# A two-layer decoder trunk: the last down group of the first layer in direct form

## The chip, the cores and the metric

The kernel runs on one core of a Trainium2 chip. The metric is the device time in microseconds (us) of one execution. Five engines work side by side, each through its own queue in order: TensorE (PE; PEld is its weight load), VectorE (DVE), ScalarE (ACT), GpSimd (POOL) and SyncE (SP), which here issues DMAs.

## The reference

512 tokens, 1024 features, two layers. Each layer adds an attention and an MLP to the residual x, all in float32:

```
for layer in range(2):
    h = rms_norm(x, g_mix[layer])
    x = x + even_mixer(...) if layer == 0 else x + odd_mixer(h, w_in_odd, b_forget, ...)
    h = rms_norm(x, g_mlp[layer])
    x = x + square(relu(h @ w_up[layer])) @ w_down[layer]
```

w_up is 1024 x 4096 and w_down 4096 x 1024. rms_norm divides each token by the root of its mean square and multiplies by a gain per feature. The odd mixer projects h to queries, keys, values (16 heads of 64) and 16 forget logits per token, whose cumulated log-sigmoid is added to the attention logits.

## The kernel before, in words

All is kept transposed: features on the 128 partitions, the 512 tokens along the free axis. The residual is four tiles `accs` of two feature chunks each. Every float32 product is made of three matmuls (`mm3`, L163 to L169): an operand is split into a rounded part (hi, a copy on ScalarE) and a remainder (lo, a subtraction on VectorE), and hi x hi, lo x hi and hi x lo are added up in PSUM.

The MLP (`mlp`, L730) works through `items`, and each item through positions. An up unit `("U", u)` computes 256 of the 4096 hidden features: four positions (two output halves by two halves of the input features) of 12 matmuls of 512 columns. A down group `("D", g, dp)` multiplies four finished units with one block of 256 output features. It uses a Strassen-like scheme of seven products (`ORDER`, L857): each operand is cut into 2 x 2 blocks, sums of blocks are formed for the weights (`ws`, L840) and for the units (`t_sums`, L773), and seven products of half width (256 columns) take the place of eight. Three of them add up in one bank, Y, from which VectorE adds into the residual after each product (`combine`, L923), and ScalarE copies the first product, X, into Y (L929). The items run: units 0 to 4, group 0, units 5 to 8, group 1, units 9 to 12, group 2, units 13 to 15, group 3.

In both layers the last group takes three units, and the last unit (`NL` = 1) is multiplied whole at the end: in the first layer chunk by chunk (L1052), six matmuls for each of the eight chunks. There each chunk is added to the residual (L1062), squared for the token sums of the next rms_norm (`squares`, L587; the adds of the first five on GpSimd, later ones on VectorE), scaled and split as the next layer's input (L1065), and stored to DRAM (L1068). `token_sums` (L596) then adds over the features by matmuls with ones, and `col_stats` (L137) makes the root's inverse `rcol`, a chain of small VectorE operations. The next layer's first projection (`vf_c`, L562: V of the first heads and the forget logits, 96 matmuls of 272 columns) uses the input without the token's scale; `forget` (L707) and V multiply by `rcol` after it.

The MLP's own rms_norm is applied late as well. `ssum` holds the mean square of each token; the residual is multiplied by it (`SCALE`, positions 12 to 18, L1002), the unscaled hidden features are squared and multiplied down, and near the end `ssum` is replaced by its reciprocal (L1006, position 4 of the last block of group 2) and the residual multiplied back (L1004), the last unit being scaled on its own (L950, GpSimd).

What sets the order: the loop at L1029 issues for each position its matmuls, the end of the position before, the split of weights six positions ahead (`prep`, R = 6), and what `todo` holds for that position (`at`, with the offsets in `FIN`, `FIND` and `FINL` after a unit, `plan`, L983). Weights are loaded eight positions ahead by SP (`early`, L860) into four buffers. Inside the MLP, VectorE, ScalarE, GpSimd and the first matmul of each step are held to program order (`pin`); elsewhere a planner orders each engine's queue by its own forecast of when operands are ready, with the program's order as priority. `load_w` (L179) loads and splits weights outside the items, on engines given by a pattern such as `PAT_ATT` (GpSimd, GpSimd and VectorE) or `PAT_START` (ScalarE and VectorE).

Of the kernel before, what the change touches and what calls it, by code (L numbers as in the profile page):

```python
# [9 lines left out]
F32 = mybir.dt.float32  # L10
# [34 lines left out]
XL = ((0, 0, 256), (0, 256, 512), (1, 0, 512), (1, 0, 0))  # L45
RPOS = (-8, 4)
SQP = 5
VENG = 'g'
SC2 = (11, 16, 26, 29)
SENG = ('vv', 'vv', 'vv', 'gg')  # L50
SENG_W = 'vvvv'
# [8 lines left out]
FIND = (0, 3, 7, 12, 17)  # L60
SCALE = (12, 14, 16, 18)
PINS = 'pgva'
TENG = 'vvvv'
# [10 lines left out]
def trunk(ctx, tc, x, g_mix, g_mlp, w_in_even, a_q_gain, a_k_gain, b_q_gain, b_k_gain, b_sinks,  # L74
# [117 lines left out]

    def layer_attention(li, hT, w_in, w_out):


        with ExitStack() as c2:
# [10 lines left out]

            def project(cols, use, ahead=False):

# [5 lines left out]
                for k0 in range(0, DC, kw):  # L215
                    srcs, o = [], 0
                    for a, b in cols:
                        srcs.append((0, o, w_in[k0 * P:(k0 + kw) * P, a:b]))
                        o += b - a
                    ws = load_w(srcs, w, kw, PAT_START if ahead else PAT_ATT)  # L220
                    if ahead:
# [288 lines left out]
            if li == 0:  # L510
                def qk_a(g):
                    return project([(g * 256, g * 256 + 256), (512 + g * 256, 512 + g * 256 + 256)], qk_use(g, 8), g == 0)

# [41 lines left out]
            else:  # L555
# [6 lines left out]
                def vf_c():  # L562
                    def use(outs):
                        forget(ap, outs)
                        v_use(0, 0)(outs)
                    return project([(2048, 2304), (3072, 3088)], use)

# [5 lines left out]

                all_of(vf_c())
                all_of(qk_c(0))
# [154 lines left out]
    def mlp(li, accs, attention_end, last):  # L730
# [5 lines left out]
        with ExitStack() as c2:  # L736
# [12 lines left out]
            def sca(m):  # L749
                pin("a", m)  # L750
# [56 lines left out]
            for g in range(NS):  # L807
                items.append(("U", 4 * g + 4))
                items += [("D", g, dp) for dp in range(4)]
                items += [("U", 4 * g + u) for u in range(5, 8)]  # L810
            items += [("D", NS, dp) for dp in range(4)]
            pos, first = [], []
            for j, it in enumerate(items):
                first.append(len(pos))
                pos += [(j, p) for p in range(4 if it[0] == "U" else 7)]
            NP = len(pos)
# [3 lines left out]
            def load(j):  # L820
                if j in raws or j >= len(items):
                    return
                it = items[j]
                raws[j] = [wp.tile([P, 4, 256], F32, tag="wraw", bufs=RAW, name="wraw") for _ in range(2)]
                for h in range(2):
                    if it[0] == "D":
                        src = wd[h, :, 4 * it[1]:4 * it[1] + nk(j), it[2] * 256:it[2] * 256 + 256]
                    else:
                        src = w_up[li, h * 512:(h + 1) * 512, it[1] * 256:it[1] * 256 + 256].rearrange(
                            "(k p) c -> p k c", p=P)  # L830
                    nc.sync.dma_start(raws[j][h][:, :nk(j)], src)

            def nk(j):

                return 4 - NL if items[j][:2] == ("D", NS) else 4

# [31 lines left out]
            def prep(n):  # L868
                if n >= NP:
                    return  # L870
                j, p = pos[n]
                if items[j][0] == "U":
                    src = quarter(j, (11, 12, 21, 22)[p])
                else:
                    i = ORDER[p][0]
                    src = quarter(j, i) if i > 10 else ws(j, i)
# [15 lines left out]
            def up_end(j, p):  # L892
                if p == 0:
                    res[j] = mp.tile([P, 2, 512], F32, tag="u", bufs=2, name="u")
                if p % 2:
                    sca(nc.scalar.activation(res[j][:, p // 2], res[j, p - 1], AF.Relu))  # L896

            def product(j, p, hi, lo):
# [36 lines left out]
            def unit_end(j):  # L935
# [7 lines left out]

                if u >= 16 - NL:
                    def whole(e):
                        s = slot("s")
                        halves(s[:, 0], s[:, 1], v[:, e])
                        store[u, e] = s

                    def scaled(e):  # L950
                        if not last:
                            scale(v[:, e], VENG)
                    return [square, lambda: scaled(0), lambda: scaled(1), lambda: whole(0), lambda: whole(1)]

# [28 lines left out]
            def plan(j):  # L983

                if items[j][0] == "D":
                    return
                u = items[j][1]
                n0 = first[j + 1]
                offs = FINL[u - 15 + NL] if u >= 15 - NL else FIND if u % 4 == 0 and u else FIN
                for i, f in enumerate(unit_end(j)):  # L990
                    at(n0 + offs[i], f)
# [9 lines left out]
            for dp in range(4):  # L1001
                at(SCALE[dp], lambda dp=dp: scale_residual(dp, SCENG[dp]))  # L1002
                if not last:
                    at(first[-4] + SC2[dp], lambda dp=dp: scale_residual(dp, SENG[dp]))  # L1004
            if not last:
                at(first[RPOS[0]] + RPOS[1], lambda: vec(nc.vector.reciprocal(ssum, ssum)))  # L1006

            def end(n):
                if n < 0:
                    return  # L1010
                j, p = pos[n]
                (up_end if items[j][0] == "U" else combine)(j, p)
                if n + 1 == NP or pos[n + 1][0] != j:
                    plan(j)

            early(0)
            npre = [0]
# [11 lines left out]
            for n, (j, p) in enumerate(pos):  # L1029
                early(n + R + LS)  # L1030
                hi, lo = ready.pop(n)
                (up if items[j][0] == "U" else product)(j, p, hi, lo)
                end(n - 1)
# [10 lines left out]
            ss = [store[u, e] for u in range(16 - NL, 16) for e in range(2)]  # L1044
            if last:
                down_last(li, accs, ss, r2col)
                return None

            ssum2 = mp.tile([P, 2, 512], F32, tag="u", bufs=2, name="ssum2")[:, 0]
            nh = []  # L1050
            r0 = FF // P - 2 * NL
            for c in range(DC):  # L1052
                if c % 4 == 0:
                    ws = []
                    for k in range(0, 2 * NL, 2):
                        ws += load_w([(0, 0, w_down[li, (r0 + k) * P:(r0 + k + 2) * P, c * P:(c + 4) * P])], 512, 2, PAT_MLP)
                o = bank("pB", "dn")
                cw = slice(c % 4 * P, c % 4 * P + P)
                for f in range(2 * NL):
                    mm3(o, ws[f][0][:, cw], ws[f][1][:, cw], ss[f][:, 0], ss[f][:, 1], f == 0, f == 2 * NL - 1, f == 0)  # L1060
                a = accs[c // 2][:, c % 2]
                nc.vector.tensor_add(a, o, a)  # L1062
                squares(c, a, ssum2, sq_pool, SQP)
                h = slot("hn")
                scale_split(h[:, 0], h[:, 1], a, gcol[:, 8 * (li + 1) + c:8 * (li + 1) + c + 1])  # L1065
                nh.append(h)
                if c % 2:
                    nc.scalar.dma_start(xsp[c // 2], accs[c // 2])  # L1068

            col_stats(token_sums(ssum2))  # L1070
            return nh

# [29 lines left out]
    accs, end = layer_attention(0, [], w_in_even[0], w_out_even[0])  # L1102
    hT = mlp(0, accs, end, False)
    accs, end = layer_attention(1, hT, w_in_odd[0], w_out_odd[0])
    mlp(1, accs, end, True)
# [22 lines left out]
```

## Time and profile before

| | us |
|---|---|
| median of 3 runs (lowest, highest) | 1203.42 (1201.02, 1204.06) |
| the profiled execution, its own time | 1202.71 |
| its span (first to last instruction) | 1200.7 |
| TensorE busy | 1165.1 |
| VectorE busy | 919.2 |
| ScalarE busy | 653.0 |
| GpSimd busy | 232.5 |

Busy times are of one execution. Durations of matmuls overlap, since they are pipelined; what a matmul costs TensorE is the distance from its start to the next one's. The granted clock (PEclk) is the share of TensorE's full clock of 2.4 GHz; the lower level is 1.2 GHz. The whole execution has a mean of 0.992.

### The profile page before, as it was taken

The page shows a single profiled execution, that of the slowest core. Times are in us where ns is not written, and L with a number is a line of the kernel's source. Part 1 is how long each engine was busy: PE and PEld are TensorE (multiplying, and loading weights), DVE is VectorE, ACT ScalarE, POOL GpSimd, SP SyncE. Part 2 cuts the span into 40 slices and gives each one's busy share as a digit, 9 for nine tenths or more (in the row PEclk, how much of TensorE's full clock was granted, in tenths as well). Part 3 has the DMA queues.
Part 4 walks back from the last instruction along what each step waited for, and adds up shares of the span by engine and source line. Part 5 has one row for each costly group of instructions (what it writes and reads, how often), then busy time and mean ns, then how long its engine had stood idle before and what let it go on. Part 6 is the DMA issues. An engine that isn't in the chain of part 4 may idle for free.

```text
span 1200.7 us, 19302 instructions
## 1 busy us (share of the span) xinstructions
PE 1165.1 (97%) x7014; PEld 1027.8 (86%) x7014; DVE 919.2 (77%) x2018; ACT 653.0 (54%) x1369; POOL 232.5 (19%) x327
## 2 busy tenths in 40 slices
PE   8799989999999999998899999999999999999998
PEld 7687887888988989988787888888889989989897
DVE  4887899868848858859947877778879668569575
ACT  6255876665545555445425675656755465455453
POOL 2445444200000000000755435332100000000000
PEclk9899999999999999999999999999999999999999
DMA  7342115232332332322543433343332422323322
GB/s 248 105 118 75 36 36 158 71 123 71 101 110 89 103 109 88 106 66 85 168 124 97 108 105 106 99 124 114 100 97 74 123 88 90 106 87 106 110 70 85
DMA packets 105718, 122.48 MB, mean 102 GB/s; under 512 B 6120, under 2 KB 94216, under 8 KB 105624
## 3 DMA queue, kind: packets, MB, share of 16 engines
q1 hardware_dynamic: 104440, 117.03, 32.6%
q0 software_dynamic: 576, 2.10, 0.5%
q10 hardware_dynamic: 608, 2.13, 0.4%
q8 instruction: 55, 0.90, 0.3%
q14 instruction: 39, 0.32, 0.1%
HBM read 108.10 MB, written 6.32 MB: 95 GB/s over the span
## 4 chain that ended last, share of the span: by engine, by line
PE 80%; DVE 10%; DMA 3%; issue 3%; POOL 2%; ACT 2%; SPq 0%; POOLq 0%; ACTq 0%; DVEq 0%
PE up L165 10%; PE up L168 10%; PE up L169 10%; PE pj L232 4%; PE pj L234 4%; PE pj L233 4%; PE Y L917 3%; PE Y L920 3%; PE Y L921 3%; PE O L383 3%; PE Z L917 2%; PE Z L921 2%; PE Z L920 2%; PE PT L363 2%; PE X L921 2%
## 5 line engine op out<-in xcount | busy, mean ns | idle before, releaser
L165 PE MATMUL up<-xin,whi 128*128 128x512 f32 x512 | 200.2, 391 | 0.0
L168 PE MATMUL up<-xin,wlo 128*128 128x512 f32 x512 | 199.7, 390 | 0.0
L169 PE MATMUL up<-xin,whi 128*128 128x512 f32 x512 | 199.5, 390 | 0.0
L759 DVE TENSOR_TENSOR wlo<-wraw,whi 128x512 fp32r<-128x512 f32 (+1 forms) x224 | 148.9, 675 | 64.3 <-ACT whi L758 59.9
L758 ACT CAST whi<-wraw 128x512 fp32r<-128x512 f32 (+1 forms) x224 | 135.3, 608 | 114.2 <-PE up L169 50.1
L758 ACT CAST whi<-s 128x512 fp32r<-128x512 f32 (+1 forms) x128 | 75.8, 593 | 76.2 <-PE Y L921 38.0
L169 PEld LDWEIGHTS up<-xin,whi 128*128 128x128 f32 x512 | 96.4, 188 | 20.2
L165 PEld LDWEIGHTS up<-xin,whi 128*128 128x128 f32 x512 | 96.5, 188 | 20.0 <-issue 0.2
L168 PEld LDWEIGHTS up<-xin,wlo 128*128 128x128 f32 x512 | 96.4, 188 | 20.0 <-issue 0.2
L917 PE MATMUL Y<-t,whi 128*128 128x256 f32 x360 | 103.2, 287 | 5.0 <-DVE acc L933 5.0
L920 PE MATMUL Y<-t,wlo 128*128 128x256 f32 x360 | 102.1, 284 | 0.0
L921 PE MATMUL Y<-t,whi 128*128 128x256 f32 x360 | 102.1, 284 | 0.0
L343 ACT ACTIVATE P<-P,negm 128x128 f32<-128x128 f32 (+5 forms) x128 | 69.6, 544 | 52.5 <-DVE negm L340 48.8
L153 POOL TENSOR_SCALAR whi<-wraw 128x512 fp32r<-128x512 f32 (+1 forms) x104 | 71.4, 690 | 122.0 <-PE pj L234 79.9
L896 ACT ACTIVATE u<-up 128x512 f32<-128x512 f32 x64 | 38.3, 599 | 101.9 <-PE up L169 101.9
L232 PE MATMUL pj<-whi,hn 128*128 128x512 f32 (+2 forms) x256 | 89.2, 348 | 0.0
L233 PE MATMUL pj<-wlo,hn 128*128 128x512 f32 (+2 forms) x256 | 87.6, 342 | 0.0
L234 PE MATMUL pj<-whi,hn 128*128 128x512 f32 (+2 forms) x256 | 87.4, 342 | 0.0
L759 DVE TENSOR_TENSOR wlo<-s,whi 128x512 fp32r<-128x512 f32 (+1 forms) x128 | 82.3, 648 | 3.1 <-ACT whi L758 3.1
L156 POOL TENSOR_TENSOR wlo<-wraw,whi 128x512 fp32r<-128x512 f32 (+1 forms) x56 | 73.4, 1314 | 21.0 <-ACT whi L151 17.8
L232 PE MATMUL pj<-whi,h 128*128 128x512 f32 (+1 forms) x192 | 68.3, 360 | 8.0 <-ACT sq L250 4.8
L917 PEld LDWEIGHTS Y<-t,whi 128*128 128x128 f32 x360 | 69.1, 192 | 6.1 <-DVE acc L933 5.8
(201 smaller groups left out, 3190.0 us busy)
## 6 DMA issues: line engine op xcount, KB each, us to landing
wraw<-in_w_up SPq DMA_DIRECT2D x64, 512.0 KB, 3.7
wraw<-in_w_down SPq DMA_DIRECT2D x52, 512.0 KB, 3.8
wraw<-in_w_in_odd SPq DMA_DIRECT2D x36, 256.0 KB, 3.0
K<-K SPq DMA_DIRECT2D x26, 256.0 KB, 2.9
wraw<-in_w_down SPq DMA_DIRECT2D x16, 384.0 KB, 3.7
wraw<-in_w_in_even SPq DMA_DIRECT2D x10, 512.0 KB, 3.7
wraw<-in_w_in_even SPq DMA_DIRECT2D x16, 256.0 KB, 4.5
xl<-xsp SPq DMA_DIRECT2D x8, 512.0 KB, 3.3
```

The source lines that it names most:

```text
L156: in_order((nc.gpsimd if lo == "pool" else nc.vector).tensor_sub(dst_l, src, dst_h.bitcast(F32)))
L165: m = nc.tensor.matmul(o, wh, xh, start=start, stop=False, skip_group_check=more)
L168: nc.tensor.matmul(o, wl, xh, start=False, stop=False, skip_group_check=more)
L169: nc.tensor.matmul(o, wh, xl, start=False, stop=stop, skip_group_check=more)
L232: nc.tensor.matmul(o, xh, hi[:, :n], start=k == 0, stop=False)
L233: nc.tensor.matmul(o, xh, lo[:, :n], start=False, stop=False)
L234: nc.tensor.matmul(o, xl, hi[:, :n], start=False, stop=k == DC - 1)
L758: sca(nc.scalar.copy(dst_h, src))
L759: late.append(lambda: vec(nc.vector.tensor_sub(dst_l, src, dst_h.bitcast(F32))))
L917: m = nc.tensor.matmul(o, wh, b(0), start=start, stop=False, skip_group_check=more)
L920: nc.tensor.matmul(o, wl, b(0), start=False, stop=False, skip_group_check=more)
L921: nc.tensor.matmul(o, wh, b(1), start=False, stop=stop, skip_group_check=more)
```

## The change

In the first layer the last group becomes four items of a new kind, `"E"`: a product of all four units (12 to 15) with a block of 256 output features in direct form, four positions of 12 matmuls of 512 columns. Its end (`direct_end`) finishes each chunk as soon as it is whole. Units 12 to 15 are not cut into blocks but squared, scaled by the reciprocal on VectorE and split whole (`part`), unit 15 in two halves as they come. The separate last unit is gone. `ssum` is inverted at position 22 (`RPL`), and the residual is multiplied back at positions 1, 3, 5 and 7 after the start of unit 13 (`SC3`), all on VectorE. The token sums and `col_stats` are handed to the next layer as a function, `stats`, which is called after three steps (`STATS`) of its first projection; that projection's weights are split on ScalarE and VectorE. The second layer's MLP stays as it was.

```diff
+FIN12 = (0, 5)
+RPL = 22
+SC3 = (1, 3, 5, 7)
+STATS = 3
...
-                    return project([(2048, 2304), (3072, 3088)], use)
+                    return project([(2048, 2304), (3072, 3088)], use, PAT_START)
...
-                all_of(vf_c())
+                g = vf_c()
+                for _ in range(STATS):
+                    next(g)
+                stats()
+                all_of(g)
                 all_of(qk_c(0))
...
-            items += [("D", NS, dp) for dp in range(4)]
+            items += [("D" if last else "E", NS, dp) for dp in range(4)]
...
-                pos += [(j, p) for p in range(4 if it[0] == "U" else 7)]
+                pos += [(j, p) for p in range(7 if it[0] == "D" else 4)]
...
-                return 4 - NL if items[j][:2] == ("D", NS) else 4
+                return 4 - NL if last and items[j][:2] == ("D", NS) else 4
...
+            def direct(j, p, hi, lo):
+
+                if p % 2 == 0:
+                    res[j, p] = bank(("pA", "pB")[j % 2], "dn")
+                o = res[j, p - p % 2]
+                for k in range(4):
+                    v = store[12 + k, p % 2]
+                    mm3(o, hi[:, k], lo[:, k], v[:, 0], v[:, 1], p % 2 == 0 and k == 0, bool(p % 2 and k == 3), k == 0)
+
+            def direct_end(j, p):
+
+                if p % 2 == 0:
+                    return
+                dp = items[j][2]
+                c = 2 * dp + p // 2
+                a = accs[dp][:, p // 2]
+                if c == 0:
+                    res["ssum2"] = consts.tile([P, 512], F32, tag="ssum", name="ssum2")
+                vec(nc.vector.tensor_add(a, res[j, p - 1], a))
+                h = slot("hn")
+                g = gcol[:, 8 * (li + 1) + c:8 * (li + 1) + c + 1]
+                sca(nc.scalar.activation(h[:, 0], a, AF.Copy, scale=g))
+                vec(nc.vector.scalar_tensor_tensor(h[:, 1], a, g, h[:, 0].bitcast(F32), op0=OP.mult, op1=OP.subtract))
+                squares(c, a, res["ssum2"], sq_pool)
+                hn.append(h)
+                if c % 2:
+                    nc.scalar.dma_start(xsp[dp], accs[dp])
...
+                def whole(e):
+                    s = slot("s") if u < 15 or last else mp.tile([P, 2, 512], F32R, tag="t24", bufs=2, name="s")
+                    halves(s[:, 0], s[:, 1], v[:, e])
+                    store[u, e] = s
...
+                def part(e):
+
+                    sca(nc.scalar.activation(v[:, e], v[:, e], AF.Square))
+                    scale(v[:, e], "v")
+                    whole(e)
+                    if u == 15:
+                        catch_up()
+
+                if not last and u >= 12:
+                    return [lambda: part(0), lambda: part(1)]
...
-                offs = FINL[u - 15 + NL] if u >= 15 - NL else FIND if u % 4 == 0 and u else FIN
+                if not last and u >= 12:
+                    offs = FIN12 if u == 12 else (0, 1)
+                else:
+                    offs = FINL[u - 15 + NL] if u >= 15 - NL else FIND if u % 4 == 0 and u else FIN
...
-                    at(first[-4] + SC2[dp], lambda dp=dp: scale_residual(dp, SENG[dp]))
+                    at(first[-7] + SC3[dp], lambda dp=dp: scale_residual(dp, "vv"))
             if not last:
-                at(first[RPOS[0]] + RPOS[1], lambda: vec(nc.vector.reciprocal(ssum, ssum)))
+                at(RPL, lambda: vec(nc.vector.reciprocal(ssum, ssum)))
...
+                if not last and items[j] == ("U", 15):
+                    if p % 2:
+                        unit_end(j)[p // 2]()
...
-            ssum2 = mp.tile([P, 2, 512], F32, tag="u", bufs=2, name="ssum2")[:, 0]
...
-            col_stats(token_sums(ssum2))
-            return nh
+            return hn, lambda: col_stats(token_sums(res["ssum2"]))
...
-    hT = mlp(0, accs, end, False)
-    accs, end = layer_attention(1, hT, w_in_odd[0], w_out_odd[0])
+    hT, stats = mlp(0, accs, end, False)
+    accs, end = layer_attention(1, hT, w_in_odd[0], w_out_odd[0], stats)
```

## Rows read from the trace of the kernel before

**Rows 1.** The page's first part: busy time, share of the span and instructions of each engine.

```profile
PE 1165.1 (97%) x7014; PEld 1027.8 (86%) x7014; DVE 919.2 (77%) x2018; ACT 653.0 (54%) x1369; POOL 232.5 (19%) x327
```

**Rows 2.** TensorE's waits between 440 and 640 us: who waited for whom, us in total, times, the longest.

```profile
PE Y L917 <- DVE acc L933: 5.0, 4, 1.9
PE pc L600 <- DVE ssum L594: 4.2, 1, 4.2
PE pz L715 <- DVE fz L711: 0.7, 1, 0.7
```

**Rows 3.** Windows of 10 us: busy us and instructions of each engine, granted clock, DMA share, GB/s.

```profile
500.00:510.00 10.00, 8.22 (x50) 7.52 (x49) 8.24 (x11) 2.60 (x5) 0.00 (x0) 0.83 0.36 105
...
550.00:560.00 10.00, 7.75 (x63) 7.35 (x62) 10.00 (x19) 4.56 (x10) 2.85 (x2) 1.00 0.30 92
...
590.00:600.00 10.00, 5.79 (x37) 5.58 (x37) 8.66 (x14) 2.16 (x4) 5.61 (x8) 0.76 0.51 161
```

**Rows 4.** The timeline of TensorE at the borders of the last group, the last unit, the first projection and the forget gate: start, us, engine, line, operation, output and inputs, idle time before and its releaser.

```profile
541.33 0.28 PE L910 MATMUL Y<-b,whi 128*128 128x256 f32 x1
...
576.16 0.40 PE L165 MATMUL dn<-s,whi 128*128 128x512 f32 x1
...
587.07 0.28 PE L232 MATMUL pj<-whi,hn 128*128 128x272 f32 x1
...
592.71 0.28 PE L232 MATMUL pj<-whi,hn 128*128 128x272 f32 x1
597.20 1.87 PE L600 MATMUL pc<-ones,ssum 128*128 128x1 f32 x8 [4.21 <-DVE ssum L594]
...
606.53 0.28 PE L234 MATMUL pj<-whi,hn 128*128 128x272 f32 x1
...
607.86 0.28 PE L715 MATMUL pz<-ident,fz 128*16 128x128 f32 x1 [0.75 <-DVE fz L711]
```

**Rows 5.** The timelines of VectorE and TensorE at the reciprocal, end of group 2 and start of unit 13.

```profile
501.88 3.35 DVE L1006 RECIPROCAL ssum<-ssum 128x512 f32<-128x512 f32 x1
...
503.50 0.28 PE L921 MATMUL X<-b,whi 128*128 128x256 f32 x1
505.56 0.39 PE L917 MATMUL Y<-t,whi 128*128 128x256 f32 x1 [1.78 <-DVE acc L933]
...
508.06 0.63 PE L168 MATMUL up<-xin,wlo 128*128 128x512 f32 x1
508.49 0.63 PE L169 MATMUL up<-xin,whi 128*128 128x512 f32 x1
...
510.03 0.39 PE L165 MATMUL up<-xin,whi 128*128 128x512 f32 x1
```

**Rows 6.** The timelines of VectorE and TensorE in group 0, around position 22 and in the block after it.

```profile
299.00 0.68 DVE L851 TENSOR_TENSOR s<-wraw 128x512 f32<-128x512 f32 x1
299.60 0.41 DVE L933 TENSOR_TENSOR acc<-Y,acc 128x256 f32<-128x256 f32 x1
...
310.61 0.42 DVE L933 TENSOR_TENSOR acc<-Y,acc 128x256 f32<-128x256 f32 x1
...
312.82 0.42 DVE L933 TENSOR_TENSOR acc<-Y,acc 128x256 f32<-128x256 f32 x1 [0.26 <-PE Y L921]
...
300.74 0.28 PE L917 MATMUL Y<-t,whi 128*128 128x256 f32 x1
...
301.46 0.28 PE L917 MATMUL Y<-t,whi 128*128 128x256 f32 x1
...
311.08 0.39 PE L917 MATMUL Y<-t,whi 128*128 128x256 f32 x1
```

**Rows 7.** The timelines of GpSimd and VectorE while GpSimd scales the last unit, and one VectorE operation of the same shape after it.

```profile
551.80 2.85 POOL L796 TENSOR_TENSOR u<-u,ssum 128x512 f32<-128x512 f32 x2 [319.87 <-ACT u L942]
...
551.94 1.58 DVE L759 TENSOR_TENSOR wlo<-wraw,whi 128x384 fp32r<-128x384 f32 x1
553.45 1.61 DVE L851 TENSOR_TENSOR s<-wraw 128x384 f32<-128x384 f32 x1
...
555.32 0.54 DVE L759 TENSOR_TENSOR wlo<-s,whi 128x384 fp32r<-128x384 f32 x1
```

**Rows 8.** The timeline of VectorE from the token sums to `rcol`, first and last and a long one, and TensorE's token sums in the second layer's MLP.

```profile
599.11 0.16 DVE L140 TENSOR_SCALAR msv<-pc 128x4 f32<-128x4 f32 x1 [1.30 <-PE pc L600]
...
601.21 1.14 DVE L134 TENSOR_TENSOR rsq<-rsq 128x4 f32<-128x4 f32 x1
...
606.12 0.16 DVE L135 SCALAR_TENSOR_TENSOR rcol<-rsq 128x4 f32<-128x4 f32 x1
...
883.15 0.95 PE L600 MATMUL pc<-ones,ssum 128*128 128x1 f32 x8
```

**Rows 9.** VectorE's groups between 251 and 588 us: line, operation, count, busy us and mean ns of one, idle before.

```profile
L794 DVE TENSOR_TENSOR acc<-acc,ssum 128x512 f32<-128x512 f32 x14 | 9.6, 722 | 0.0
...
L1062 DVE TENSOR_TENSOR acc<-dn,acc 128x512 f32<-128x512 f32 x6 | 4.0, 682 | 0.8 <-PE dn L169 0.8
```

**Rows 10.** VectorE's timeline at the first products of group 2.

```profile
467.23 0.42 DVE L933 TENSOR_TENSOR acc<-Z,acc 128x256 f32<-128x256 f32 x1 [0.56 <-PE Z L921]
```

**Rows 11.** TensorE's waits between 606 and 885 us, the longest.

```profile
PE S L326 <- DMA K<-K: 2.8, 3, 1.2
```

More of the change, by code (lines that the diff above doesn't have):

```diff
@@ L45 @@
 XL = ((0, 0, 256), (0, 256, 512), (1, 0, 512), (1, 0, 0))
-RPOS = (-8, 4)
 SQP = 5
-VENG = 'g'
-SC2 = (11, 16, 26, 29)
-SENG = ('vv', 'vv', 'vv', 'gg')
 SENG_W = 'vvvv'
@@ L191, in load_w, with layer_attention @@
         return res
-    def layer_attention(li, hT, w_in, w_out):
+    def layer_attention(li, hT, w_in, w_out, stats=None):
         with ExitStack() as c2:
@@ L206, in layer_attention, with project @@
             nc.gpsimd.memset(p3[:, :, 256:384].bitcast(F32), 0.0)
-            def project(cols, use, ahead=False):
+            def project(cols, use, pat=PAT_ATT, ahead=False):
                 n = sum(b - a for a, b in cols)
@@ L219, in project @@
                         o += b - a
-                    ws = load_w(srcs, w, kw, PAT_START if ahead else PAT_ATT)
+                    ws = load_w(srcs, w, kw, pat)
                     if ahead:
@@ L511, in qk_a @@
                 def qk_a(g):
-                    return project([(g * 256, g * 256 + 256), (512 + g * 256, 512 + g * 256 + 256)], qk_use(g, 8), g == 0)
+                    return project([(g * 256, g * 256 + 256), (512 + g * 256, 512 + g * 256 + 256)], qk_use(g, 8),
+                                   *((PAT_START, True) if g == 0 else ()))
                 def v_a(g):
@@ L825, in load @@
                 for h in range(2):
-                    if it[0] == "D":
+                    if it[0] != "U":
                         src = wd[h, :, 4 * it[1]:4 * it[1] + nk(j), it[2] * 256:it[2] * 256 + 256]
@@ L871, in prep @@
                 j, p = pos[n]
-                if items[j][0] == "U":
+                if items[j][0] != "D":
                     src = quarter(j, (11, 12, 21, 22)[p])
@@ L942, in square @@
                         sca(nc.scalar.activation(v[:, e], v[:, e], AF.Square))
[L944 to L953, printed above, removed]
+                def whole(e):
+                    s = slot("s") if u < 15 or last else mp.tile([P, 2, 512], F32R, tag="t24", bufs=2, name="s")
+                    halves(s[:, 0], s[:, 1], v[:, e])
+                    store[u, e] = s
+                if last and u >= 16 - NL:
+                    return [square, lambda: None, lambda: None, lambda: whole(0), lambda: whole(1)]
+                def part(e):
[6 more added lines that the diff above has]
+                    return [lambda: part(0), lambda: part(1)]
                 def tsum():
@@ L983, in plan @@
             def plan(j):
-                if items[j][0] == "D":
+                if items[j][0] != "U":
                     return
@@ L1011, in end @@
                 j, p = pos[n]
-                (up_end if items[j][0] == "U" else combine)(j, p)
-                if n + 1 == NP or pos[n + 1][0] != j:
+                {"U": up_end, "D": combine, "E": direct_end}[items[j][0]](j, p)
+                if not last and items[j] == ("U", 15):
+                    if p % 2:
+                        unit_end(j)[p // 2]()
+                elif n + 1 == NP or pos[n + 1][0] != j:
                     plan(j)
+            hn = []
             early(0)
@@ L1031, in mlp @@
                 hi, lo = ready.pop(n)
-                (up if items[j][0] == "U" else product)(j, p, hi, lo)
+                {"U": up, "D": product, "E": direct}[items[j][0]](j, p, hi, lo)
                 end(n - 1)
@@ L1043, in mlp @@
                 catch_up()
-            ss = [store[u, e] for u in range(16 - NL, 16) for e in range(2)]
             if last:
-                down_last(li, accs, ss, r2col)
+                down_last(li, accs, [store[u, e] for u in range(16 - NL, 16) for e in range(2)], r2col)
                 return None
-            ssum2 = mp.tile([P, 2, 512], F32, tag="u", bufs=2, name="ssum2")[:, 0]
[L1050 to L1068, printed above, removed]
-            col_stats(token_sums(ssum2))
-            return nh
+            return hn, lambda: col_stats(token_sums(res["ssum2"]))
     def down_last(li, accs, ss, r2col):
```

## The prediction

> **What bounds the kernel now.** I read the page first: TensorE is busy 97% of the span [rows 1], so time can only come out of TensorE's pauses, its low-clock stretches, or its matmul count. The waits of TensorE between 440 and 640 us, which cover the end of the first layer's MLP and the start of the next projections, then show 9.9 us of pauses in six waits: four for VectorE's adds into the residual, one for VectorE's last token-sum add, one for the forget gate [rows 2]. The windows show where: 500 to 510, 550 to 560 and 590 to 600 us have TensorE busy for 8.2, 7.8 and 5.8 us of 10, the granted clock being 0.83, 1.00 and 0.76 [rows 3]. The timeline of TensorE gives the borders of each piece [rows 4], and VectorE's shows what it was doing while TensorE waited.
>
> Two pitches price all matmuls. One of 512 columns takes (541.33 - 510.03) / 138 = 0.227 us [rows 4, 5]; one of 256 takes (301.46 - 300.74) / 6 = 0.120 us [rows 6].
>
> **Part 1: the last down group in direct form.** It removes the last group's 4 x 7 products (four blocks of 4 x 7 x 9 = 252 matmuls of 256 columns, and 4 initial ones) and the last unit's 8 x 6 = 48 matmuls of 512, and adds 4 x 4 x 12 = 192 of 512. In work that is 256 x 0.120 + 48 x 0.227 = 41.6 us before and 192 x 0.227 = 43.6 us after: 2.0 us more. In time, group and last unit took 587.07 - 541.33 = 45.7 us [rows 4], as 4.1 us were lost to waits and late weights. So this piece gains 2.1 us if the new one runs without a pause.
>
> Does it? In the product form VectorE adds every product into the residual while the next but one accumulates in the same bank, so a late add stops TensorE. The direct form has an add at the end of a chunk only (0.68 us [rows 9]), and that bank is used again two items later, some 20 us. An item of four positions loads, splits and uses weights as an up unit does, and the up units from 510 to 541 us ran at the bare pitch. VectorE's work for an item is four weight remainders, two adds, two remainders of the next layer's input and two token-sum adds, ten operations of about 0.7 us: 7 us beside 10.9 us of matmuls. The units' scaling moves from GpSimd to VectorE (eight multiplies of 0.7 us [rows 9]) and lies beside up units. The sharpest date is the last unit's second half: relu, square, multiply, copy, subtract, five operations of 0.6 to 0.7 us, 3.2 us, against 12 + 9 matmuls = 4.8 us before it is read. I cost it at nothing; without that cover it is 3.2 us.
>
> On the multiply there is a row for the shared cost: GpSimd's two multiplies (551.80, 2.85 us) made two VectorE operations take 1.58 and 1.61 us, where the same shape takes 0.54 [rows 7], and TensorE's longest wait for an add, 1.9 us, follows [rows 2]. This goes, and VectorE's own multiplies come in a stretch where it has room.
>
> A page speaks against the direct form's arithmetic. The Trainium skill, "TensorE: Matmul & The Clock Gate", section "Wait — 56ns, not 53.3ns?", puts a warm matmul at its columns over 2.4 GHz and 2.5 ns more, 215.7 ns for 512; by it halves and wholes cost the same per column, and the replaced pieces would cost 38.3 us and the new one 41.4: 3.1 us more work instead of 2.0, though the new piece itself would be 2.2 us shorter than mine and the kernel would end near 1193.3. The pitches measured here, 227 and 120 ns, hold 13 and 11 ns more than that, and the measurement decides.
>
> **Part 2: chunks finished one by one, token sums inside the next projection.** Before, the last unit's eight chunks came every 1.36 us (six matmuls), faster than VectorE and GpSimd finished them, so a backlog stood when they ended. The projection ran 45 pitches from 587.07 to 592.71 (0.125 us each), then TensorE stood 4.2 us for the last token-sum add, did the sums at the low clock, and ended at 606.66 [rows 4]: 19.6 us. After, a chunk takes 24 matmuls, 5.4 us, against some 3 us of VectorE, so only the last chunk is open when the direct form ends: add, copy, remainder, square and sum, about 3.3 us. Its token sums stand behind three of the projection's blocks, 36 x 0.125 = 4.5 us. So no wait; 96 x 0.125 = 12.0 us and 0.95 us for the sums at the full clock [rows 8]: 13.0 us, a gain of 6.6 us. The last chunk is read only after six blocks, 9 us. The V and forget weights lose GpSimd's splits and take ScalarE and VectorE (eight times about 0.4 us, beside the direct form, free).
>
> The next date is the column scale: from the sums to rcol took 606.28 - 599.07 = 7.2 us [rows 8]; after, the sums end 5.5 us into the projection, rcol comes at 12.7 and the projection ends at 13.0. That is as tight as before, so the forget gate's 0.7 us wait [rows 4] stays. Parts 1 and 2: -2.1 - 6.6 = -8.7 us.
>
> **Part 3: the reciprocal moves from the end of the third group to position 22, the third product of the first group.** It is one VectorE operation of 3.35 us [rows 5]. At its old place TensorE's next product, due at 503.62, started at 505.56, and the clock fell afterwards: the seventh up matmul began at 510.03 where 503.62 + 1.44 + 6 x 0.227 = 506.42 was due. This 3.6 us goes. At the new place it stands before the operation of 299.00 us [rows 6]. Behind it in VectorE's order is the add of 299.60, for which TensorE's Y product of 300.74 waits: 3.3 us later, a pause of 2.4. And VectorE has no idle time until 312.8 us; the add of 310.61 already holds the matmul of 311.08 back by 0.1 us [rows 6]. So the whole 3.2 us comes through. What the low clock adds there is between nothing (550 to 560 us, a wait of 1.9 us, clock 1.00 [rows 2, 3]) and 1.7 us (as at 505 us, 3.6 less the pause of 1.9); I take 0.8. Sum of part 3: -3.6 + 4.0 = +0.4.
>
> **Part 4: the units of the last group are finished whole.** Units 12 to 14 drop the block sums and two of their splits and gain a multiply. For unit 12 this falls at the third group's first product: ScalarE's copy of the half waits for VectorE's multiply, and behind it on ScalarE stands the X-to-Y copy which the third product needs. VectorE has 0.56 us idle there [rows 10]; one multiply, one remainder and the wait overrun it by about 0.5 us. Bounds 0 and 1.3 (two operations at 0.68); I take 0.5, the nearest being that idle row. The residual's eight multiplies come 12 to 20 us earlier, beside units 13 and 14. Loads: the same 4 MB in pieces of 512 KB with the same lookahead of eight positions on SP's queue; the next layer's weights stand behind them in the same order as now.
>
> **Sum.** -8.7 + 0.4 + 0.5 = -7.8 us. The profiled execution took 1202.71 us, so 1194.9; the median of runs lies 0.7 us above it, so I predict 1195.6 us.
>
> **Rivals.**
> - *The backlog stays.* If the last sums still come after TensorE is there, part 2's 6.6 us are not won: 1202.2. For it: the matmuls of the token sums stood first in the program before too and ran after 46 projection matmuls, so the program's place isn't the queue's place. Against: the backlog came from chunks every 1.36 us. 13%.
> - *rcol late.* GpSimd, free of the V weights, starts splitting the query and key weights sooner, beside the column scale's dozen tiny operations. Two of them took 1.14 us for 4 elements while GpSimd subtracted [rows 8], where others take 0.16. Three more such hits are 3 us of TensorE waiting at the forget gate, 1198.6. 15%. The Trainium skill, "SBUF — State Buffer", section "SBUF: two separate sides", has the two engines share a port pair that one holds for a whole instruction; by that rule each hit may cost a whole GpSimd instruction, and the trace agrees with 1.14 us.
> - *Slower: the first group falls to the low clock and stays.* Position 22 makes TensorE pause at several Y products in a row. At the low level a 256-column matmul takes about 0.21 us (0.43 for 512 [rows 5]) instead of 0.12; 34 us of products remain after 301 us, and would take 60: 1195.6 + 22 = 1218. It passes the old time by 0.3% once the low level lasts some 27 us. Against it: the low stretch after the pause at 505 us was over by 510.03 us [rows 5]. 7%.
> - *Better:* no low clock in the first group, no overrun in the third, rcol sooner: -2.4, 1193. 10%.
>
> My forecast has 55%; its own range is 1193 to 1198. The next layer's attention has 2.8 us of waits of one kind between 606 and 885 us [rows 11] and few others, so another order of its instructions can only lose there, 1 to 3 us. The range is 1190.5 to 1201.5: below, all doubts falling well; above, the backlog mostly staying. Faster by over 0.3% (below 1199.8; less than that a measurement can't tell from no change): forecast, better and most of late rcol, 80%. Within: backlog and a rest, 13%. Slower: 7%.
>
> **What would show it.** Right: the direct form's 192 matmuls in 43.5 to 44 us; no wait for the token sums, projection ends 13 to 14 us after it; a wait for an add near 300 us of 2 to 3 us, and 3 us more in the first group; none near 505. Wrong: a wait of several us before the token sums, pauses between chunks, or up units slower than the pitch.

## The result, and the profile after

The changed kernel takes 1193.52 us (median of 5 runs, 1192.46 to 1194.07), the kernel before in the same batches 1204.06 (1201.02 to 1204.72). The ratio is 0.9926, with a 95% interval of 0.9907 to 0.9945. So the time is lower by 0.55 to 0.93%. The forecast was 1195.6, with a range of 1190.5 to 1201.5 and 80% on a time lower by more than 0.3%. The profiled execution's span went from 1200.7 to 1191.2 us.

The first part of the page, busy us of each engine, answers to [rows 1]:

```profile
PE 1162.3 (98%) x6902; PEld 1020.3 (86%) x6902; DVE 893.1 (75%) x1962; ACT 646.0 (54%) x1351; POOL 212.1 (18%) x307
```

TensorE has 112 matmuls less (256 + 48 were replaced by 192) and lost only 2.8 us of busy time; VectorE lost 26. TensorE's waits of the first layer's MLP and the second layer's attention, 240 to 900 us (who waited for whom, us in all, times, longest), answer to [rows 2] and [rows 11]:

```profile
PE S L326 <- DMA K<-K: 2.9, 3, 1.2
PE Y L950 <- DVE acc L966: 2.6, 2, 2.4
PE Y L950 <- ACT Y L962: 0.4, 1, 0.4
```

The 4.2 us for the token sums are gone, the forget gate's 0.7 too, and all four waits for VectorE's adds of [rows 2]: the one behind the reciprocal in group 2 and the three of the last group. What is left for adds is new and lies elsewhere: the timelines of VectorE and TensorE in group 0 show it, as the answer to [rows 5] and [rows 6].

```profile
298.66 3.35 DVE L1050 RECIPROCAL ssum<-ssum 128x512 f32<-128x512 f32 x1
301.92 0.63 DVE L856 TENSOR_TENSOR s<-wraw 128x512 f32<-128x512 f32 x1
302.47 0.41 DVE L966 TENSOR_TENSOR acc<-Y,acc 128x256 f32<-128x256 f32 x1
...
302.93 0.39 PE L950 MATMUL Y<-t,whi 128*128 128x256 f32 x1 [2.38 <-DVE acc L966]
```

The add that started at 299.60 us in the kernel before starts at 302.47 here, behind the reciprocal and a weight sum, and the Y product behind it pauses for 2.38 us.

The timeline of TensorE at the borders, the answer to [rows 4], says what each piece takes:

```profile
294.53 0.28 PE L943 MATMUL Y<-b,whi 128*128 128x256 f32 x1
...
338.76 0.40 PE L165 MATMUL up<-xin,whi 128*128 128x512 f32 x1
...
466.89 0.28 PE L943 MATMUL Y<-b,whi 128*128 128x256 f32 x1
...
509.08 0.40 PE L165 MATMUL up<-xin,whi 128*128 128x512 f32 x1
...
541.75 0.39 PE L165 MATMUL dn<-s,whi 128*128 128x512 f32 x1
...
585.27 0.28 PE L232 MATMUL pj<-whi,hn 128*128 128x272 f32 x1
...
598.19 0.49 PE L720 MATMUL pz<-ident,fz 128*16 128x128 f32 x3
...
599.10 0.39 PE L234 MATMUL pj<-whi,hn 128*128 128x512 f32 x1
```

The starts of the kernel before that [rows 4] doesn't have; the last is the third matmul of the query and key projection:

```profile
294.87 0.28 PE L910 MATMUL Y<-b,whi 128*128 128x256 f32 x1
...
335.90 0.40 PE L165 MATMUL up<-xin,whi 128*128 128x512 f32 x1
...
464.03 0.28 PE L910 MATMUL Y<-b,whi 128*128 128x256 f32 x1
...
507.63 0.63 PE L165 MATMUL up<-xin,whi 128*128 128x512 f32 x1
...
606.69 0.42 PE L715 MATMUL pz<-ident,fz 128*16 128x128 f32 x2
...
608.74 0.39 PE L234 MATMUL pj<-whi,hn 128*128 128x512 f32 x1
```

The table subtracts such starts in both kernels.

| piece, us on TensorE | before | after | difference | forecast |
|---|---|---|---|---|
| group 0 | 41.03 | 44.23 | +3.20 | +4.0 |
| group 2 | 43.60 | 42.19 | -1.41 | |
| units 13 to 15 | 33.70 | 32.67 | -1.03 | |
| group 2 and units together | 77.30 | 74.86 | -2.44 | -3.1 |
| last group and last unit, or direct form | 45.74 | 43.52 | -2.22 | -2.1 |
| first projection with the token sums | 19.62 | 12.92 | -6.70 | -6.6 |
| forget gate to the third matmul after | 2.05 | 0.91 | -1.14 | 0 |
| sum | | | -9.30 | -7.8 |

From there to the second layer's MLP both take 243.63 us and from there to the last matmul 344.1 us: nothing downstream changed. Another 0.34 us lies ahead of the MLP (its first matmul starts at 239.57 and 239.23 us), where no line was changed, so the last matmul comes 9.64 us earlier; behind it 0.1 us comes back, which makes the span's 9.5. What lies ahead varies between executions: over all the profiles below, group 0 starts anywhere from 293.68 to 296.25 us.

The VectorE row of the last chunk shows the order that the prediction put down for it:

```profile
585.47 0.69 DVE L921 TENSOR_TENSOR acc<-dn,acc 128x512 f32<-128x512 f32 x1 [1.82 <-PE dn L169]
...
586.95 0.75 DVE L925 SCALAR_TENSOR_TENSOR hn<-acc,gcol,hn 128x512 fp32r<-128x512 f32 x1 [0.44 <-ACT hn L924]
587.62 0.68 DVE L599 TENSOR_TENSOR ssum<-ssum,sqx 128x512 f32<-128x512 f32 x1
...
595.62 0.47 DVE L135 SCALAR_TENSOR_TENSOR rcol<-rsq 128x4 f32<-128x4 f32 x1
```

VectorE waits for TensorE here (1.82 us idle), not the other way; the last sum ends 3.0 us after the direct form, at 588.30. The token sums start 1.5 us later without a wait:

```profile
589.78 0.94 PE L605 MATMUL pc<-ones,ssum 128*128 128x1 f32 x8
```

### The profile page after: what moved, and what is told of

The parts are those of the page before. It is cut to its first block, busy times and chain, and to the rows that moved or that the text cites. A ratio compares the mean times of both kernels' runs of the same rounds, so it can differ in the third digit from the quotient of the medians.

```text
span 1191.2 us, 18927 instructions
## 1 busy us (share of the span) xinstructions
PE 1162.3 (98%) x6902; PEld 1020.3 (86%) x6902; DVE 893.1 (75%) x1962; ACT 646.0 (54%) x1351; POOL 212.1 (18%) x307
## 4 chain that ended last, share of the span: by engine, by line
PE 81%; DVE 10%; DMA 3%; issue 2%; ACT 2%; POOL 1%; SPq 0%; ACTq 0%; POOLq 0%; DVEq 0%
PE up L165 10%; PE up L168 10%; PE up L169 10%; PE pj L232 4%; PE pj L234 4%; PE pj L233 4%; PE Y L950 3%; PE Y L953 3%; PE Y L954 3%; PE O L383 2%; PE Z L950 2%; PE X L953 2%; PE X L950 2%; PE Z L954 2%; PE Z L953 2%; PE X L954 2%
## 5 line engine op out<-in xcount | busy, mean ns | idle before, releaser
L763 ACT CAST whi<-wraw 128x512 fp32r<-128x512 f32 (+1 forms) x228 | 138.7, 613 | 106.4 <-PE up L169 48.3
L764 DVE TENSOR_TENSOR wlo<-wraw,whi 128x512 fp32r<-128x512 f32 (+1 forms) x228 | 152.1, 679 | 56.5 <-ACT whi L763 54.3
L763 ACT CAST whi<-s 128x512 fp32r<-128x512 f32 (+1 forms) x112 | 67.6, 604 | 70.0 <-PE Y L954 35.0
L950 PE MATMUL Y<-t,whi 128*128 128x256 f32 x324 | 92.7, 286 | 3.0 <-DVE acc L966 2.6
L953 PE MATMUL Y<-t,wlo 128*128 128x256 f32 x324 | 91.7, 283 | 0.0
L954 PE MATMUL Y<-t,whi 128*128 128x256 f32 x324 | 91.6, 283 | 0.0
L153 POOL TENSOR_SCALAR whi<-wraw 128x512 fp32r<-128x512 f32 x96 | 65.8, 687 | 140.7 <-PE pj L234 118.3
L764 DVE TENSOR_TENSOR wlo<-s,whi 128x512 fp32r<-128x512 f32 (+1 forms) x112 | 73.7, 663 | 2.4 <-ACT whi L763 2.4
L232 PE MATMUL pj<-whi,h 128*128 128x512 f32 (+1 forms) x192 | 68.5, 361 | 6.9 <-DVE v L161 3.1
L156 POOL TENSOR_TENSOR wlo<-wraw,whi 128x512 fp32r<-128x512 f32 x52 | 69.7, 1344 | 21.8 <-ACT whi L151 18.7
L234 PE MATMUL pj<-whi,h 128*128 128x512 f32 (+1 forms) x192 | 66.6, 348 | 0.0
```

The source lines that it names most:

```text
L156: in_order((nc.gpsimd if lo == "pool" else nc.vector).tensor_sub(dst_l, src, dst_h.bitcast(F32)))
L232: nc.tensor.matmul(o, xh, hi[:, :n], start=k == 0, stop=False)
L234: nc.tensor.matmul(o, xl, hi[:, :n], start=False, stop=k == DC - 1)
L763: sca(nc.scalar.copy(dst_h, src))
L764: late.append(lambda: vec(nc.vector.tensor_sub(dst_l, src, dst_h.bitcast(F32))))
L950: m = nc.tensor.matmul(o, wh, b(0), start=start, stop=False, skip_group_check=more)
```

## Experiments

**The reciprocal in an up unit.** Of the changed kernel:

```diff
-RPL = 22
+RPL = 50
```

> The reciprocal moves from position 22 (first group) to position 50, the third position of unit 5. Theory: in a down group every add into the residual is waited for, so VectorE's 3.35 us come through to TensorE; in an up unit nobody waits for VectorE within 3 us. The first group then takes 40.9 us instead of 44.1, no wait for an add near 300 us, and the time falls by 3.2 us, to 1190.3. Rival: VectorE has no room anywhere in these stages, the 3.3 us only move to unit 5 or the second group: the time stays at 1193.5.

1190.91 us (median of 4), ratio to the kernel before 0.9893 (0.9873 to 0.9914). The profile has no wait for an add in the first group, and group 0 took 336.82 - 295.78 = 41.04 us:

```profile
295.78 0.28 PE L943 MATMUL Y<-b,whi 128*128 128x256 f32 x1
...
336.82 0.40 PE L165 MATMUL up<-xin,whi 128*128 128x512 f32 x1
```

VectorE's timeline in unit 5 shows why it is free there: it had waited 1.78 us for ScalarE before, and 0.94 after.

```profile
340.43 0.69 DVE L764 TENSOR_TENSOR wlo<-wraw,whi 128x512 fp32r<-128x512 f32 x1 [1.78 <-ACT whi L763]
341.04 3.35 DVE L1050 RECIPROCAL ssum<-ssum 128x512 f32<-128x512 f32 x1
...
345.87 0.69 DVE L764 TENSOR_TENSOR wlo<-wraw,whi 128x512 fp32r<-128x512 f32 x1 [0.94 <-ACT whi L763]
```

From the end of group 0 to the start of group 2 both kernels take 128.1 us. So the 3.2 us of part 3 are shown, and the rival, that they only move, is out. The median fell by 2.6 us, not 3.2, and its interval overlaps that of the changed kernel: it is the group's time that shows the gain. In the profiled execution group 0 began 1.25 us later than after the change, ahead of every changed line.

**The same in the kernel before.**

```diff
-                at(first[RPOS[0]] + RPOS[1], lambda: vec(nc.vector.reciprocal(ssum, ssum)))
+                at(50, lambda: vec(nc.vector.reciprocal(ssum, ssum)))
```

> The kernel before, with only the reciprocal moved, to the third position of unit 5. Theory: at its old place it cost a pause of 1.9 us and the low clock after it, 3.6 us in all, and at the new place nothing: the third group takes 41.0 us instead of 43.6, unit 13 starts at full clock, time lower by 3.6 us, about 1200. Rival: the low clock there wasn't the pause's doing and stays, 1.9 us won.

1200.06 us (median of 10) beside 1202.87, ratio 0.9975 (0.9964 to 0.9987). Group 2 took 41.04 us and units 13 to 15 32.67:

```profile
465.45 0.28 PE L910 MATMUL Y<-b,whi 128*128 128x256 f32 x1
...
506.49 0.40 PE L165 MATMUL up<-xin,whi 128*128 128x512 f32 x1
...
539.16 0.28 PE L910 MATMUL Y<-b,whi 128*128 128x256 f32 x1
```

That is 2.56 + 1.03 = 3.59 us less, the 3.6 of part 3, low clock included. The median fell by 2.8. In the profiled execution 0.8 us of the gain went again at the pause near 553 us, where this time the clock fell (window 550 to 560, granted clock 0.83; 1.00 in [rows 3]); how often it does so in the other runs isn't known:

```profile
550.00:560.00 10.00, 8.15 (x55) 7.95 (x55) 9.26 (x17) 3.49 (x9) 2.47 (x2) 0.83 0.32 92
```

**Unit 12 finished beside unit 13.** Of the changed kernel:

```diff
-FIN12 = (0, 5)
+FIN12 = (28, 30)
```

> Unit 12 is squared, scaled and split at the first and third position of unit 13 instead of at the first and sixth position of the third group. Theory: the third group's 42.2 us (40.9 for the second) come from ScalarE, whose X-to-Y copy stands behind a copy that waits for VectorE's multiply; with both gone from the group it takes 41.0 us and the time falls by 1.1 us, to 1192.4. Rival: the same work beside units 12 and 13 delays the direct form's operands or the weights: the group gets shorter, but as much is lost in units 13 to 15, time 1193.5.

1191.99 us (median of 4), ratio 0.9911 (0.9895 to 0.9926). Group 2 took 507.13 - 466.34 = 40.79 us, 1.40 less than after the change, and units 13 to 15 took 32.67 us as after the change: nothing was lost there in return.

```profile
466.34 0.28 PE L943 MATMUL Y<-b,whi 128*128 128x256 f32 x1
...
507.13 0.40 PE L165 MATMUL up<-xin,whi 128*128 128x512 f32 x1
```

With `FIN12 = (0, 5)` VectorE's and ScalarE's timelines at the start of group 2 read:

```profile
468.76 0.69 DVE L799 TENSOR_TENSOR u<-u,ssum 128x512 f32<-128x512 f32 x1 [3.04 <-ACT u L987]
...
469.49 0.62 ACT L763 CAST s<-u 128x512 fp32r<-128x512 f32 x1 [0.76 <-DVE u L799]
...
470.43 0.39 PE L950 MATMUL Y<-t,whi 128*128 128x256 f32 x1 [0.39 <-ACT Y L962]
```

VectorE's multiply stood 3.04 us idle for ScalarE's square; ScalarE's copy then waited 0.76 us for the multiply, and the X-to-Y copy behind it held TensorE for 0.39. The rest of the 1.40 us are gaps of 0.1 to 0.5 us at this product and at later ones of the group.

**Both moves.** `RPL = 50` and `FIN12 = (28, 30)`.

> Both moves together. Theory: the two losses are of different places and add up: 1193.5 - 3.2 - 1.1 = 1189.2. Rival: they overlap, VectorE's or ScalarE's order shifts the waits elsewhere, and no more than 3 us are won: 1190.5 or above.

1187.48 us (median of 4, 1186.44 to 1191.31), ratio 0.9881 (0.9861 to 0.9900): faster than both kernels, since its interval and that of the changed kernel (0.9907 to 0.9945) don't meet. Group 0 took 41.05 us and group 2 40.79, so the two gains add up, to 4.6 us. The profiled execution took 1188.27 us, 4.7 less than that of the changed kernel (1192.98), which fits; the median's 6.0 us are more than the two explain. Between 240 and 900 us TensorE then waits 2.5 us for the keys of the attention and 0.5 us for its transposed probabilities, and for nothing of the MLP:

```profile
PE S L326 <- DMA K<-K: 2.5, 3, 1.2
```

**The place of the token sums in the program.** Of the changed kernel:

```diff
-STATS = 3
+STATS = 0
```

> The token sums and the column scale are asked for before the next projection instead of after three of its steps. Theory: the planner orders TensorE's queue by its own forecast, so the sums go behind two blocks instead of three and the last add is just there: a wait of 0 to 0.5 us, time within 0.5 us of 1193.5. Rival: the place in the program is what removed the wait; the sums then stand first and TensorE waits some 3 us for the last chunk, at the low clock afterwards: 1197 or more.

1194.14 us (a single run), 0.6 above the median of the changed kernel; there is no wait for the sums, and from the projection's start to the third matmul after the forget gate 600.45 - 586.43 = 14.02 us against 13.83. The planner had put the sums behind two blocks, 24 matmuls. And the other way round, in the kernel before:

```diff
-            col_stats(token_sums(ssum2))
-            return nh
+            return nh, lambda: col_stats(token_sums(ssum2))
...
+                g = vf_c()
+                for _ in range(3):
+                    next(g)
+                stats()
```

> The kernel before, with nothing changed but that the token sums and the column scale are handed to the next layer and asked for after three steps of its first projection. Theory: the wait came from the backlog of chunks and the planner had put the sums behind 46 matmuls already, so nothing changes: the wait for the sums stays at 4 us or so, time within 1 us of 1203. Rival: the new place in the program is worth several us: 1198 or less.

1203.86 us (a single run), beside 1202.87 for the kernel before, and the wait was 5.0 us:

```profile
PE pc L604 <- DVE ssum L598: 5.0, 1, 5.0
```

So the other part of the change, the token sums asked for inside the next projection, is worth nothing by itself.

**Chunks finished at the end.** The chunk's add stays where it is; its copy, remainder, square and sum are issued after the last chunk:

```diff
                 vec(nc.vector.tensor_add(a, res[j, p - 1], a))
+                open_chunks.append((c, dp, a))
...
             end(NP - 1)
             catch_up()
+            for f in open_chunks:
+                finish_chunk(*f)
```

> The direct form stays, and each chunk is still added to the residual as it comes, but the copies, remainders, squares and sums of all eight chunks are issued after the last one. Theory: what removes the wait for the token sums is that only one chunk is open at the end. With eight open, VectorE needs eight times 1.3 us for them, the sums come some 10 us after the direct form and the column scale 5 us later, while the projection is done after 13: TensorE loses 4 to 7 us, time 1197 to 1201. Rival: the planner hides it behind the projection, which needs the chunks one by one only every 1.5 us: time within 1 us of 1193.5.

1195.41 us (a single run). The loss behind the direct form was 0.74 us (14.57 against 13.83), another 0.74 in group 0, which has to do with the clock (below). This would speak for the rival, but VectorE's timeline shows that the experiment did not do what it was to do: after the add of chunk 6 (581.77) a remainder and a sum follow as in the changed kernel, and only three of the eight remainders come behind the last add (587.21).

```profile
581.77 0.69 DVE L921 TENSOR_TENSOR acc<-dn,acc 128x512 f32<-128x512 f32 x1 [1.82 <-PE dn L169]
...
583.25 0.75 DVE L931 SCALAR_TENSOR_TENSOR hn<-acc,gcol,hn 128x512 fp32r<-128x512 f32 x1 [0.44 <-ACT hn L930]
...
587.82 2.07 DVE L931 SCALAR_TENSOR_TENSOR hn<-acc,gcol,hn 128x512 fp32r<-128x512 f32 x3
```

It says only that the program's order didn't set when a chunk is finished. So the backlog was forced by a dependence:

```diff
+                z = accs[3][:, 1]
+                vec(nc.vector.scalar_tensor_tensor(held[:, :8], z[:, :8], 0.0, gcol[:, 8:16], op0=OP.mult, op1=OP.add))
+                vec(nc.vector.tensor_scalar(held[:, 8:9], z[:, :1], 0.0, 1.0, op0=OP.mult, op1=OP.add))
...
-                g = gcol[:, 8 * (li + 1) + c:8 * (li + 1) + c + 1]
+                g = held[:, c:c + 1]
...
-                squares(c, a, res["ssum2"], sq_pool)
+                squares(c, a, res["ssum2"], sq_pool, scale=held[:, 8:9])
```

> As the changed kernel, but the scale of the next layer's input and that of the squares are read from a small tile which is written only after the last chunk's add (its value plus 0 times that chunk), so that all eight chunks are finished after the direct form, whatever the planner forecasts. Theory: a backlog of eight chunks is 8 x 1.3 us on VectorE; the projection starts 1 to 3 us late, the token sums come 11 to 13 us after the direct form instead of 4.5, the column scale 5 us after them, and TensorE loses 4 to 6 us against the changed kernel: 1197.5 to 1199.5. Rival: the projection eats the chunks as fast as they come and hides it: 1 us or less.

1208.5 us (a single run), slower than the kernel before (1201.24). From the direct form's start to the third matmul after the forget gate it took 613.67 - 541.67 = 72.00 us, against 57.35 after the change: 14.65 us lost, about three times the forecast.

```profile
541.67 0.39 PE L165 MATMUL dn<-s,whi 128*128 128x512 f32 x1
...
613.67 0.63 PE L234 MATMUL pj<-whi,hn 128*128 128x512 f32 x1
```

TensorE's waits, and the windows behind the direct form:

```profile
PE pz L720 <- DVE fz L716: 4.6, 1, 4.6
...
PE pc L605 <- DVE ssum L599: 2.2, 1, 2.2
PE pj L232 <- ACT hn L931: 2.0, 1, 2.0
PE pj L234 <- DVE hn L932: 0.9, 1, 0.9
```

```profile
600.00:610.00 10.00, 5.48 (x23) 5.16 (x23) 7.09 (x17) 0.00 (x0) 3.84 (x5) 0.66 0.53 159
610.00:620.00 10.00, 8.34 (x26) 6.27 (x27) 6.49 (x16) 4.44 (x8) 1.45 (x2) 0.66 0.18 56
```

The waits are 9.7 us, and (second fence, granted clock in the third column from the end) for much of the 20 us from 600 to 620 TensorE runs at the low clock (0.66). VectorE's remainders took 1.09 us and some sums 1.77 instead of 0.75 and 0.69 as long as GpSimd was splitting the next weights; how much of the loss is GpSimd's was not tried. What is shown: with all eight chunks held back, GpSimd's splits beside them included, 14.65 us are lost, and the change would be a loss. All eight open is more than the kernel before had at that point, so the figure is no measure of its own backlog.

**GpSimd's part.** In the kernel before, the scaling alone:

```diff
-VENG = 'g'
-SENG = ('vv', 'vv', 'vv', 'gg')
+VENG = 'v'
+SENG = ('vv', 'vv', 'vv', 'vv')
```

> The kernel before, with the last unit and the last residual block scaled on VectorE instead of GpSimd. Theory: GpSimd's multiplies held VectorE for 2 us near 552 us and made TensorE wait 1.9 us; without them this wait is gone, and another microsecond at the chunks: 1200 to 1201.5. Rival: the multiplies cost VectorE 0.6 us each in a stretch where it is full, and the wait only changes its name: within 0.5 us of the time before.

1204.54 us (a single run) beside 1202.87: no gain. The wait of 1.85 us at 555.45 is gone, so GpSimd's multiplies had made it; but that of 0.97 us at 565.00 became 2.17 at 564.33:

```profile
564.33 0.39 PE L917 MATMUL Y<-t,whi 128*128 128x256 f32 x1 [2.17 <-DVE acc L933]
```

In all, the waits of the last group fell from 3.2 to 2.6 us, and the clock took that back (560 to 570 us: 0.83, before 1.00), so that group and unit took 46.33 us against 45.74. The rival held as to the time: VectorE was full there, with or without GpSimd. Then all of it, with the token-sum adds on VectorE (`SQP = 0`) and the V and forget weights on ScalarE and VectorE:

> The kernel before, with GpSimd taken out of its end altogether: the last unit's and the residual's scaling and all token-sum adds on VectorE, the V and forget weights split on ScalarE and VectorE. Theory: the backlog is one of rate. Eight chunks come in 10.9 us and are 8 x 1.9 us of VectorE even without GpSimd in its way, with the weights' remainders 18 us, so TensorE still waits 2 to 5 us for the token sums and the time stays within 1.5 us of the one before. Rival: GpSimd's slow adds and its hold on VectorE made the backlog: the wait is gone and the time falls by 4 us or more.

1201.52 us beside 1201.24 (single runs): the time is as the theory had it, but not by the wait that it named.

```profile
PE pj L233 <- DVE wlo L156: 1.7, 2, 1.1
PE pc L600 <- DVE ssum L594: 0.6, 1, 0.6
```

The wait for the sums fell from 4.2 to 0.6 us, so GpSimd's work did set that one: not its scaling, without which the wait was still 4.6 us, but its adds or its weight splits, which weren't tried apart. TensorE then waited for the weights' remainders on VectorE, part of it at the low clock (0.80 from 590 to 600 us): the projection and what follows took 607.61 - 587.96 = 19.65 us, where the kernel before took 21.67 and the changed one 13.83. Of the 7.84 us between these, 2.0 come from GpSimd's work alone; the other 5.8 come only with the direct form, whose chunks are further apart. And in the changed kernel the V weights back on GpSimd (`project` without `PAT_START`):

> The changed kernel with the V and forget weights split as before, mostly on GpSimd. Theory: VectorE has room beside the direct form and the last sum has 1.5 us to spare, so it costs nothing: within 0.7 us of 1193.5, no wait for the token sums over 0.5 us. Rival: GpSimd holds VectorE in the last chunk and the column scale: 2 us more.

1193.84 us (a single run), and 600.08 - 586.25 = 13.83 us behind the direct form, to the digit as with ScalarE and VectorE. That part of the change is worth nothing beside the direct form.

## Why the prediction was right

*Part 1.* Forecast -2.1, measured -2.22. The 192 matmuls ran at the bare pitch (43.52 us; 43.6 forecast) with no pause between chunks. The Trainium skill, "TensorE: Matmul & The Clock Gate", section "Wait — 56ns, not 53.3ns?", puts a warm matmul of 512 columns at 215.7 ns, an estimate of 41.4 us for the 192; the trace does not agree, its pitch is 43.52 / 192 = 0.227 us. (The prediction's "13 and 11 ns more than that" is a slip: 227 and 120 ns are both 11 ns above that page's sum.) The sum is made of two amounts of opposite sign, 2.0 us more work and 4.1 us of waits less. Its remark that GpSimd's hold on VectorE made the longest wait is borne out, but moving the multiplies alone gained nothing.

*Part 2.* Forecast -6.6, measured -6.70, sums at the predicted place, 4.5 us into the projection. The reason given, a backlog that no longer stands at the end, is borne out: with all chunks held back the waits are there again, and with GpSimd's work taken out of the kernel before, 5.8 of the 7.84 us of projection and forget gate stay. The size that the forced backlog costs was far off (4 to 6 forecast, 14.65 measured). One clause was wrong: the forget gate's wait was forecast to stay, "as tight as before", and 1.14 us went. The column scale took 596.09 - 590.72 = 5.4 us instead of 7.2; VectorE had one weight remainder among its small operations instead of two in the stretch of [rows 8], but that this is the whole cause was not tried.

*Part 3.* Old place: -3.6 forecast, 3.59 measured on its own. New place: pause 2.4 forecast, 2.38 measured; 3.2 for the group forecast, 3.20 measured. The 0.8 for the low clock did not come in this execution; in others it did (below), so that here it was luck.

*Part 4.* The mis-sized term. Forecast +0.5; group 2 took 42.19 us against 41.04 in the kernel before without its reciprocal, that is +1.15, inside its bounds of 0 to 1.3, and 1.40 came back when the work was moved away. The mechanism was right, ScalarE's copy behind VectorE's multiply; the size was not. The step that failed: VectorE's idle 0.56 us was taken as room for the multiply. The multiply can't start then: it waits for ScalarE's square, and the weight sums and remainders behind it in VectorE's queue waited those 3.04 us with it.

The terms that missed are -0.8 (clock), -1.1 (forget gate), +0.7 (part 4 with the rest of its stretch), -0.2 (parts 1 and 2) and -0.3 ahead of the MLP; together they make the 1.8 us between -7.8 and the 9.6 us by which the last matmul came earlier. The first and the last of them owe nothing to the prediction's reasoning. Of the rivals, the low clock in the first group did not come to stay, and the other two, the late column scale and the backlog, are refuted by the profile of the changed kernel. The better case, 1193 with 10%, came nearest to the time: two of its three doubts fell well, the overrun in the third group did not.

## What to carry to other kernels

Where an engine adds each partial product into a running sum in order, one long operation on it (a reciprocal of 3.35 us) can cost TensorE almost its full length (3.2 us in group 0 here); put where nobody waits for that engine, here in an up unit, it was free. Results should come no faster than they can be finished: a form with 2 us more matmuls won, for the smaller part because it has fewer adds to wait for, and for the larger mainly because its chunks come every 5.4 us instead of every 1.36. With a planner that orders queues by its own forecast, moving a call in the program may change nothing, so the queue in the trace is to be looked at before the move is credited.

## What was not expected

The same pause of 2.38 us at the same place left the clock alone in some executions and not in others. With it TensorE's granted clock from 300 to 310 us was 1.00 in the changed kernel and group 0 took 44.23 us; with the chunks issued at the end, whose group 0 is the same code, it was 0.83 and 44.97 us. Of the six profiled executions with the reciprocal at position 22, four had 1.00 there and two 0.83 (the other is the forced backlog, 45.01 us); what decides it, no run here shows.

```profile
300.00:310.00 10.00, 7.43 (x60) 7.02 (x59) 9.97 (x19) 3.74 (x8) 0.00 (x0) 1.00 0.18 55
```

```profile
300.00:310.00 10.00, 7.62 (x53) 7.42 (x52) 9.41 (x15) 2.52 (x5) 0.00 (x0) 0.83 0.23 76
```

It cost 0.74 us there and not the 1.7 of the pause at 505 us; at least 0.2 of the difference is a second wait for an add, which the changed kernel has in that group (0.20 us) and this execution has not. And the forced backlog showed a low clock that lasts: 0.66 over 20 us, in which TensorE's work came in pieces between waits.
